# Three lanes of attention blocks instead of two, with more probability and transposed tiles

## The chip, the core and the metric

The kernel runs on one core of a Trainium2 chip. The metric is the device time of one launch in microseconds (us), median of several runs; lower is better. A core has a matrix engine (TensorE, PE in the rows; its weight loads are PEld), a vector engine (VectorE, DVE), an activation engine (ScalarE, ACT), a general engine (GpSimd, POOL) and a queue that issues DMA transfers (SyncE, SP). Each takes its instructions in the order in which they were written for it; between engines they wait on semaphores.

## What is computed

Two layers on 1024 tokens of width 1024: an even layer (RWKV and DeltaNet heads), then an odd layer with chunked attention; each also has an MLP and a gated embedding. All is in 32-bit floats, and products are made three times with a high and a low part of each operand. The change touches the attention of the odd layer alone:

```python
def chunk_band_attention(h, w_qkv, q_g, k_g, rel_bias):     # 16 heads of 64, chunks of 64
    qkv = (h @ w_qkv).reshape(bsz, seq, 3, C_HEADS, C_HEAD_DIM)
    q = rmsnorm(qkv[:, :, 0], q_g) * (C_HEAD_DIM ** -0.5)
    k = rmsnorm(qkv[:, :, 1], k_g)
    v = qkv[:, :, 2]
    ...
    def one_chunk(c):                  # a chunk sees itself and the 8 chunks before it
        s = jnp.einsum('bqhd,bkhd->bhqk', q_c, k_b).astype(jnp.float32) + bias
        s = jnp.where(valid, s, -jnp.inf)
        prob = jax.nn.softmax(s, -1).astype(v.dtype)
        return jnp.einsum('bhqk,bkhd->bqhd', prob, v_b)
```

## The kernel before

The attention is cut into 16 steps (8 pairs of heads, each in two halves of 512 queries), and a step into 4 blocks: 2 heads by 2 blocks of 256 queries, 64 blocks in all. One block (`attn_block`, line 1745) goes through these stations:

- Scores, for each of its two tiles of 128 queries: TensorE writes the near keys, which have a bias that depends on distance, into a bank `sn` of its accumulation memory (PSUM; two such banks) and the far keys into `sf` (one bank). VectorE adds the bias tile `toep` and takes the maximum (line 1795, into the probability tile `pb`), reduces `sf` (L1803) and joins the maxima (L1804); ScalarE takes the exponentials (L1805, L1808); VectorE makes the reciprocal of the sum (L1811); ScalarE scales `pb` with it (L1812). There are four `pb` tiles.
- Transposition: TensorE turns `pb` piece by piece into a bank `pt` (two banks). ScalarE casts it into the high part of a tile `ptile` (L317), VectorE subtracts to get the low part (L318). There are three `ptile` tiles.
- Values: TensorE multiplies `ptile` with the values `vs` into the bank `po` (one bank). After a head's second block, ScalarE copies and VectorE adds one half to the other (L1853, L1854), and `y` is stored.

Around this, `attn_ins` makes the q, k, v products of later steps (`dps<-wq,act`, 24 matmuls of 384 columns for each of 64 tiles of tokens, two banks), and after the last step it goes on with the output projection; `attn_norms` normalizes and transposes q and k of a step.

A planner in the program (`run`, line 112) sets the order in which all this is written: every generator is a lane, and the one whose next piece is due first goes next, by a table of delays (`LAT`). Two of the lanes are `attn_lane`; both draw blocks from one list of jobs, so two blocks are under way. A block's values must follow those of the block before it (`("pv", job - 1)`). The tile framework then orders the instructions of each engine within its own limits, and makes an instruction wait when its tile is still in use.

GpSimd squares q and k (L1711) and, when the first block of a head of a new pair is written, subtracts a number from that head's bias tile `toep` and masks a corner of it (L1753, L1754). The bias tiles come by DMA into three buffers (L1679).

Of the kernel before, what the change touches and what calls it, by code (L numbers as in the profile page):

```python
# [8 lines left out]
F32 = mybir.dt.float32  # L9
F32R = mybir.dt.float32r  # L10
I32 = mybir.dt.int32
AF = mybir.ActivationFunctionType
ALU = mybir.AluOpType
# [4 lines left out]
P = 128  # L18
# [3 lines left out]
HB = 512  # L22
NT = T // P
C = 128
NEG = -1.0e30
# [79 lines left out]
class Trunk:  # L105
# [1470 lines left out]
    def layer1_in(self):  # L1576
        nc, tc, a = self.nc, self.tc, self.a
        with ExitStack() as es:
            self.psm = es.enter_context(self.pool("psml1", space=PSUM))
            wp = self.wp = es.enter_context(self.pool("l1a", 2))  # L1580
            self.wr = es.enter_context(self.pool("l1wr", 2))
            self.w1 = es.enter_context(self.pool("l1w1"))
            l1 = es.enter_context(self.pool("l1", 2))
            self.sm = es.enter_context(self.pool("sml1", 2))
            self.yd = [[self.dr.tile([P, HB], F32, tag=f"yd{k}{hf}", name="yd") for hf in range(2)] for k in range(NK)]
            rbl = l1.tile([P, 16], F32, tag="rbl", name="rbl", bufs=1)
            nc.sync.dma_start(out=rbl, in_=a["rb_last"].rearrange("(o c) -> o c", o=1).broadcast_to((P, 16)))

            steps = [(pr, hf) for pr in range(8) for hf in range(2)]
            self.st = {}  # L1590

            self.ql = [[pool.tile([P, HB], F32R, tag=tag, name="Ql", bufs=1) for pool, tag in
                        ((self.accp, f"acc{e}"), (l1, f"Ql{e}"))] for e in range(2)]
            jobs = iter([(s, h, b) for s in range(16) for h in range(2) for b in range(2)])
            self.run([self.attn_lane(steps, jobs, l1, rbl) for _ in range(2)] + [self.attn_norms(steps, l1), self.attn_ins(steps, l1)])

    def attn_ins(self, steps, l1):
        kv = {}
# [31 lines left out]
        yield from self.out_early(1, self.xd, lambda q: act([P, 2, 2, HB], F32R), xt, load_w,  # L1630
                                  [("at", 14), ("at", 14), ("at", 14), ("at", 15)])

    def attn_norms(self, steps, l1):
        K = []
        for s, (pr, hf) in enumerate(steps):
            yield ("qk", s)
            if s >= 2:
                yield ("at", s - 2)
            yield from self.attn_norm(s, self.st[s], l1)
            K = K[-1:] if hf else []  # L1640
            K = K + [self.st[s]["k"]]
            self.st[s]["K"] = K
            self.mark(("in", s), self.lat["norm"])

    def attn_lane(self, steps, jobs, l1, rbl):

        for s, h, b in jobs:
            yield ("in", s)
            yield from self.attn_block(s, *steps[s], h, b, l1, rbl)

    def weights3(self, odd):

# [89 lines left out]
            st[nm] = F  # L1742
            yield "attn_norm0"

    def attn_block(self, s, pr, hf, h, blk, l1, rbl):

        nc, psm, sm = self.nc, self.psm, self.sm
        V, A, G = nc.vector, nc.scalar, nc.gpsimd
        st = self.st[s]
        m0 = 4 * hf + 2 * blk  # L1750
        if hf == 0 and blk == 0:
            t = st["toep"][h]
            G.tensor_scalar(t, t, rbl[:, 2 * pr + h:2 * pr + h + 1], None, op0=ALU.subtract)  # L1753
            G.memset(t[0:64, 320:384], NEG)  # L1754
        hs = slice(64 * h, 64 * h + 64)
        Q, Ql, K, vs, toep = st["Q"], st["Ql"], st["K"], st["vs"], st["toep"][h]

        def score(ps, m, j0, n):
            qs = slice((m % 4) * P, (m % 4) * P + P)
            o = 0  # L1760
            while o < n:
                j = j0 + o
                e = min(n - o, 4 - j % 4)
                ks = slice((j % 4) * P, (j % 4 + e) * P)
                k = K[j // 4]
                self.mm(ps[:, o * P:(o + e) * P], Q[:, h, qs], k[:, h, ks], start=True, stop=False)
                self.mm(ps[:, o * P:(o + e) * P], Ql[h][:, qs], k[:, h, ks], start=False, stop=True)
                o += e
# [16 lines left out]
        for m in (m0, m0 + 1):  # L1785
            n0 = max(0, m - 2)
            nn = m - n0 + 1
            f0 = max(0, m - 4)
            nf = n0 - f0
            pn = psm.tile([P, HB], F32, tag="sn", name="sn", bufs=2)  # L1790
            score(pn[:, 0:nn * P], m, n0, nn)
            mx = sm.tile([P, 4], F32, tag="mx", name="mx", bufs=4)
            pb = self.wp.tile([P, 5 * P], F32, tag="pb", name="pb", bufs=4)
            S = pb[:, nf * P:(nf + nn) * P]
            V.tensor_tensor_reduce(S, pn[:, 0:nn * P], toep[:, (3 - nn) * P:], op0=ALU.add, op1=ALU.max,  # L1795
                                   scale=1.0, scalar=NEG, accum_out=mx[:, 0:1])
            l = sm.tile([P, 4], F32, tag="l", name="l", bufs=4)
            if nf:
                pf = psm.tile([P, HB], F32, tag="sf", name="sf")
                score(pf[:, 0:nf * P], m, f0, nf)  # L1800
                if m >= 4:
                    V.memset(pf[64:128, 0:64], NEG)
                V.reduce_max(mx[:, 1:2], pf[:, 0:nf * P], axis=AX.X)  # L1803
                V.tensor_scalar(mx[:, 2:3], mx[:, 0:1], mx[:, 1:2], -1.0, op0=ALU.max, op1=ALU.mult)  # L1804
                A.activation(pb[:, 0:nf * P], pf[:, 0:nf * P], AF.Exp, bias=mx[:, 2:3], accum_out=l[:, 1:2])  # L1805
            else:
                V.tensor_scalar(mx[:, 2:3], mx[:, 0:1], -1.0, None, op0=ALU.mult)
            A.activation(S, S, AF.Exp, bias=mx[:, 2:3], accum_out=l[:, 0:1])  # L1808
            if nf:
                V.tensor_tensor(l[:, 0:1], l[:, 0:1], l[:, 1:2], op=ALU.add)  # L1810
            V.reciprocal(l[:, 2:3], l[:, 0:1])  # L1811
            A.activation(pb[:, 0:(nf + nn) * P], pb[:, 0:(nf + nn) * P], AF.Copy, scale=l[:, 2:3])  # L1812
            probs.append((pb, f0))
            yield "attn_block0"
# [9 lines left out]
        for b in range(bank + 1):  # L1824
            pt = psm.tile([P, HB], F32, tag="pt", name="pt", bufs=2)
            for j, (bb, o, c0, c1) in place.items():
                if bb != b:
                    continue
                for e in range(2):
                    if c0 <= 128 * e < c1:  # L1830
                        pb, f0 = probs[e]
                        self.tr(pt[:, o + 128 * e - c0:o + 128 * e - c0 + P],
                                            pb[:, (j - f0) * P:(j - f0 + 1) * P], self.ident)
            t = self.wp.tile([P, 2, HB], F32R, tag="ptile", name="ptile", bufs=3)
            self.split_scaled(t, pt[:, 0:used[b]], None, slice(0, used[b]))
            pts.append(t)
            yield "attn_block2"
# [3 lines left out]
        for j, c0, c1 in segs:  # L1841
            b, o, _, _ = place[j]
# [111 lines left out]
```

## Time and profile before

| | us |
|---|---|
| median of 3 runs | 3196.68 (3195.02 to 3198.12) |
| the profiled execution | 3200.01 |
| its span, first to last instruction | 3198.3 |
| TensorE busy in the span | 3102.1 (97%) |
| VectorE, ScalarE, GpSimd busy | 2013.2, 1384.2, 531.5 |

The profile is of one execution; the span starts and ends with an instruction, and the 1.7 us beyond it lie around the program. Times in rows are us from the span's start, unless ns is written. A busy TensorE is not a TensorE at its peak: matmuls overlap, and the pace is read from one start to the next. The attention stands between about 1772 and 2396 us. "PEclk" is the share of TensorE's full clock that the chip granted in a stretch.

### The profile page before, as it was taken

Reading aid. Unit: us, or ns where it says so; the run is one execution under the profiler, and the core shown is the slowest. Engines: PE = TensorE matmul, PEld = TensorE weight load, DVE = VectorE, ACT = ScalarE, POOL = GpSimd, SP = SyncE. Lnnn points to the kernel's source line nnn. Section 1 sums busy time; section 2 is a strip of 40 time slices with the busy share of each in tenths; the row PEclk is TensorE's granted clock in tenths of the full one; section 3 lists DMA queues with packets and bytes.
Section 4 is the critical chain, followed back from the end, with each engine's and each line's share of the span. In section 5 each row is a group of like instructions: output and inputs, shape, how many; then the busy total and the mean of one; then the engine's idle time right before and its main releaser. Section 6 shows DMA issues by size and latency. Waiting matters only on the chain.

```text
span 3198.3 us, 46044 instructions
## 1 busy us (share of the span) xinstructions
PE 3102.1 (97%) x17576; PEld 2565.6 (80%) x17576; DVE 2013.2 (63%) x4020; ACT 1384.2 (43%) x2608; POOL 531.5 (17%) x978
## 2 busy tenths in 40 slices
PE   7999999999999999999999898999899999999999
PEld 5777777777777888888888888988778888888887
DVE  6566675556748666655546576776768666655552
ACT  4333333334326555322123477777756555312121
POOL 6334442433410000000004211010110000000002
PEclk8999899999899999999999999999999999999999
DMA  3322112212325433523213210110156433522213
GB/s 120 94 63 60 47 46 67 70 61 70 129 95 194 155 119 108 192 93 106 92 51 128 70 36 32 45 41 16 69 177 209 150 121 109 185 105 92 106 47 105
DMA packets 144716, 309.60 MB, mean 97 GB/s; under 512 B 40944, under 2 KB 43120, under 8 KB 144496
## 3 DMA queue, kind: packets, MB, share of 16 engines
q1 hardware_dynamic: 126064, 273.10, 25.6%
q10 hardware_dynamic: 18432, 33.56, 2.7%
q8 instruction: 138, 2.26, 0.3%
q14 instruction: 82, 0.67, 0.1%
HBM read 232.16 MB, written 74.45 MB: 96 GB/s over the span
## 4 chain that ended last, share of the span: by engine, by line
PE 85%; DVE 7%; ACT 3%; DMA 2%; issue 1%; POOL 0%; SPq 0%; ACTq 0%; DVEq 0%; POOLq 0%
PE dps L161 70%; PE ch L161 3%; PE iz L161 2%; PE pm L161 2%; PE tp L161 1%; PE po L161 1%; PE py L161 1%; DVE ptile L318 1%; PE pt L165 1%; DMA wraw<-in_w_qkv 1%; PE sn L161 1%; PE pp L161 1%; DVE pb L1795 1%; PE sc L161 1%; ACT pb L1808 1%
## 5 line engine op out<-in xcount | busy, mean ns | idle before, releaser
L161 PE MATMUL dps<-r,act 128*128 128x512 f32 x3528 | 824.4, 392 | 0.0
L161 PEld LDWEIGHTS dps<-r,act 128*128 128x128 f32 x3528 | 662.1, 188 | 145.7
L161 PE MATMUL dps<-xg,whi 128*128 128x512 f32 x1280 | 438.2, 418 | 11.7 <-ACT xg L320 7.3
L161 PE MATMUL dps<-late,act 128*128 128x512 f32 x1536 | 352.9, 391 | 0.0
L161 PEld LDWEIGHTS dps<-late,act 128*128 128x128 f32 x1536 | 288.4, 188 | 63.1
L161 PE MATMUL dps<-wq,act 128*128 128x384 f32 x1536 | 304.8, 344 | 5.8 <-DVE vs L1704 3.1
L1452 POOL TENSOR_TENSOR pn<-pn,prs 128x512 f32<-128x512 f32 x32 | 45.5, 1426 | 1590.7 <-ACT prs L354 1496.3
L161 PEld LDWEIGHTS dps<-xg,whi 128*128 128x128 f32 x1280 | 248.4, 199 | 75.2 <-issue 10.7
L161 PEld LDWEIGHTS dps<-wq,act 128*128 128x128 f32 x1536 | 265.6, 191 | 10.4 <-DVE vs L1704 5.1
L161 PE MATMUL dps<-xg,wlo 128*128 128x512 f32 x640 | 266.4, 416 | 3.1 <-DVE wlo L277 3.1
L1328 DVE TENSOR_TENSOR late<-late,dps 128x512 f32<-128x512 f32 x224 | 152.9, 685 | 150.1 <-PE dps L161 119.2
L1427 DVE TENSOR_TENSOR xw<-xw,dps 128x512 f32<-128x512 f32 x192 | 131.5, 685 | 148.4 <-PE dps L161 145.5
L1226 ACT CAST act<-act 128x1024 fp32r<-128x1024 f32 (+1 forms) x99 | 94.8, 964 | 285.2 <-DMA act<-in_w 124.2
L1226 ACT CAST act<-late 128x512 fp32r<-128x512 f32 x210 | 124.5, 618 | 135.9 <-PE dps L161 117.0
L1227 DVE TENSOR_TENSOR act<-late,act 128x512 fp32r<-128x512 f32 x210 | 139.9, 687 | 26.1 <-ACT act L1226 25.9
L161 PEld LDWEIGHTS dps<-xg,wlo 128*128 128x128 f32 x640 | 126.9, 198 | 34.1 <-issue 4.8
L161 PE MATMUL dps<-xw,act 128*128 128x512 f32 x576 | 138.9, 392 | 0.0
L276 ACT CAST whi<-wraw 128x1024 fp32r<-128x1024 f32 x78 | 81.7, 1047 | 124.2 <-PE dps L161 74.4
L161 PEld LDWEIGHTS dps<-xw,act 128*128 128x128 f32 x576 | 108.1, 188 | 24.1
L1227 DVE TENSOR_TENSOR act<-act 128x1024 fp32r<-128x1024 f32 (+1 forms) x99 | 109.9, 1115 | 21.0 <-ACT act L1226 19.8
L161 PE MATMUL po<-ptile,vs 128*128 128x256 f32 (+1 forms) x576 | 104.9, 297 | 17.1 <-DVE ptile L318 7.7
L277 DVE TENSOR_TENSOR wlo<-wraw,whi 128x1024 fp32r<-128x1024 f32 x78 | 101.4, 1301 | 25.6 <-ACT whi L276 25.6
(472 smaller groups left out, 5369.4 us busy)
## 6 DMA issues: line engine op xcount, KB each, us to landing
act<-in_w SPq DMA_DIRECT2D x68, 512.0 KB
hd<-late ACTq DMA_DIRECT2D x128, 256.0 KB
late<-in_w SPq DMA_DIRECT2D x60, 512.0 KB
wraw<-in_w_in SPq DMA_DIRECT2D x56, 512.0 KB
act<-hd SPq DMA_DIRECT2D x56, 512.0 KB
wraw<-in_w_out SPq DMA_DIRECT2D x21, 512.0 KB
wraw<-in_w_qkv SPq DMA_DIRECT2D x21, 512.0 KB
pn<-pnd SPq DMA_DIRECT2D x32, 256.0 KB
```

The lines of the kernel that those rows point to most:

```text
L161: return self.nc.tensor.matmul(out, lhsT, rhs, start=start, stop=stop)
L165: return self.nc.tensor.transpose(out, in_, ident)
L276: nc.scalar.copy(hi, raw)
L277: nc.vector.tensor_tensor(lo, raw, hi.bitcast(F32), op=ALU.subtract)
L318: nc.vector.tensor_tensor(dst[:, 1, sl], src, dst[:, 0, sl].bitcast(F32), op=ALU.subtract)
L1226: A.copy(hi, s)
L1227: V.tensor_tensor(lo, s, hi.bitcast(F32), op=ALU.subtract)
L1328: V.tensor_tensor(r, t, u, op=ALU.add)
L1427: V.tensor_tensor(x[n][:, sl], x[n][:, sl], ps, op=ALU.add)
L1452: G.tensor_tensor(pn, pn, prs[:, sl], op=ALU.mult)
L1795: V.tensor_tensor_reduce(S, pn[:, 0:nn * P], toep[:, (3 - nn) * P:], op0=ALU.add, op1=ALU.max, scale=1.0, scalar=NEG, accum_out=mx[:, 0:1])
L1808: A.activation(S, S, AF.Exp, bias=mx[:, 2:3], accum_out=l[:, 0:1])
```

## The change

Three lanes draw from the list of blocks. The `pb` tiles go from 4 to 6, the `ptile` tiles from 3 to 4. The memory for that comes from a reserve for descriptors of dynamic DMAs, set to 1024 bytes. The work on the two bias tiles of a pair moves from the first block of each head to `attn_norms`, where both are done when the pair's first step is normalized. Nothing is computed that was not computed before, and no instruction is added or removed.

```diff
-            self.run([self.attn_lane(steps, jobs, l1, rbl) for _ in range(2)] + [self.attn_norms(steps, l1), self.attn_ins(steps, l1)])
+            self.run([self.attn_lane(steps, jobs, l1) for _ in range(3)] + [self.attn_norms(steps, l1, rbl), self.attn_ins(steps, l1)])
...
             yield from self.attn_norm(s, self.st[s], l1)
+            for h in range(0 if hf else 2):
+                t = self.st[s]["toep"][h]
+                self.nc.gpsimd.tensor_scalar(t, t, rbl[:, s + h:s + h + 1], None, op0=ALU.subtract)
+                self.nc.gpsimd.memset(t[0:64, 320:384], NEG)
...
-        if hf == 0 and blk == 0:
-            t = st["toep"][h]
-            G.tensor_scalar(t, t, rbl[:, 2 * pr + h:2 * pr + h + 1], None, op0=ALU.subtract)
-            G.memset(t[0:64, 320:384], NEG)
...
-            pb = self.wp.tile([P, 5 * P], F32, tag="pb", name="pb", bufs=4)
+            pb = self.wp.tile([P, 5 * P], F32, tag="pb", name="pb", bufs=6)
...
-            t = self.wp.tile([P, 2, HB], F32R, tag="ptile", name="ptile", bufs=3)
+            t = self.wp.tile([P, 2, HB], F32R, tag="ptile", name="ptile", bufs=4)
...
-    nc = bacc.Bacc("TRN2", target_bir_lowering=False, num_devices=1)
+    nc = bacc.Bacc("TRN2", target_bir_lowering=False, num_devices=1,
+                   dynamic_dma_scratch_size=1024)
```

The other lines of the diff pass `rbl` to `attn_norms` instead of `attn_block`.

How this moves instructions is shown at two places. The first is TensorE at the last block of the sixth step (`pt` is a bank of transposed probabilities, `po` the bank of value products, `sn` and `sf` scores of other blocks). Before:

```order
L161 MATMUL sf<-F_18069,F_18119 128x128
L161 MATMUL sf<-F_18069,Ql 128x128
L165 MATMUL pt<-ident,pb 128x128 x6
L161 MATMUL po<-ptile,vs 128x256
L165 MATMUL pt<-ident,pb 128x128 x2
L161 MATMUL po<-ptile,vs 128x256 x7
L161 MATMUL po<-ptile,vs 128x128
L165 MATMUL pt<-ident,pb 128x128 x3
```

The first value product stands right behind the transpositions that make its tile. The same block on TensorE after the change:

```order
L165 MATMUL pt<-ident,pb 128x128 x4
L161 MATMUL sn<-F_18100,F_18119 128x128
L161 MATMUL sn<-F_18100,Ql 128x128
L161 MATMUL po<-ptile,vs 128x128
L161 MATMUL sn<-F_18100,F_18119 128x256
L161 MATMUL sn<-F_18100,Ql 128x256
L161 MATMUL po<-ptile,vs 128x128 x3
L165 MATMUL pt<-ident,pb 128x128 x4
L161 MATMUL sf<-F_18100,F_18119 128x128
L161 MATMUL sf<-F_18100,Ql 128x128
L161 MATMUL po<-ptile,vs 128x256
L165 MATMUL pt<-ident,pb 128x128 x2
```

The first four transpositions belong to the block; the 128-column value products behind them are still the block before's. Scores, those products and four more transpositions now stand between the first bank and the first product of its tile (`po` with 256 columns).

The second place is GpSimd, in the stretch where the bias tile of the second head of the fourth pair is made ready (`toep_17528` before, `toep_17552` after; `sq` is the squaring of q and k). Before:

```order
L1711 TENSOR_TENSOR sq_17848<-qk_17530 128x512
L1711 TENSOR_TENSOR sq_17851<-qk_17530 128x512
L1753 TENSOR_SCALAR toep_17528<-toep_17528,rbl_15492 128x384
L1754 MEMSET toep_17528 64x64
L1711 TENSOR_TENSOR sq_18326<-qk_17867 128x512
L1711 TENSOR_TENSOR sq_18329<-qk_17867 128x512
```

After, with the change's own line numbers:

```order
L1715 TENSOR_TENSOR sq_17908<-qk_17554 128x512
L1715 TENSOR_TENSOR sq_17911<-qk_17554 128x512
L1642 TENSOR_SCALAR toep_17552<-toep_17552,rbl_15492 128x384
L1715 TENSOR_TENSOR sq_18400<-qk_17927 128x512
L1643 MEMSET toep_17552 64x64
L1715 TENSOR_TENSOR sq_18403<-qk_17927 128x512
```

The subtraction keeps its place ahead of the next step's squares; the masking slips behind the first of them.

## Rows read from the trace of the kernel before

**Rows 1.** Busy time by stretch: attention, then rest; PE, PEld, DVE, ACT, POOL, PEclk, DMA.
```profile
1800.00:2396.00 596.00, 548.80 (x3365) 505.08 (x3364) 420.89 (x1325) 428.43 (x996) 70.89 (x69) 0.97 0.18 58
2396.00:3190.00 794.00, 794.00 (x3479) 650.22 (x3478) 477.20 (x654) 285.95 (x431) 21.67 (x16) 1.00 0.35 123
```

**Rows 2.** Who TensorE waited for, 1800 to 2396: us in total, times, longest.
```profile
PE po L161 <- DVE ptile L318: 7.7, 12, 1.6
PE po L161 <- ACT ptile L317: 6.4, 10, 1.8
PE pt L165 <- ACT pb L1812: 6.1, 9, 1.8
PE pt L165 <- DVE ptile L318: 4.8, 12, 1.0
PE sf L161 <- ACT pb L1805: 3.8, 7, 1.3
```

**Rows 3.** Timeline of all engines at one block: start, us, instruction, idle before it.
```profile
2019.13 0.88 PE L165 MATMUL pt<-ident,pb 128*128 128x128 f32 x6
...
2020.03 1.05 ACT L317 CAST ptile<-pt 128x512 fp32r<-128x512 f32 x2
2020.62 0.69 DVE L318 TENSOR_TENSOR ptile<-pt,ptile 128x512 fp32r<-128x512 f32 x1 [1.37 <-ACT ptile L317]
2020.64 0.38 PE L161 MATMUL po<-ptile,vs 128*128 128x256 f32 x1 [0.64 <-ACT ptile L317]
2021.23 0.68 DVE L1712 TENSOR_REDUCE ss<-sq 128x8 f32<-128x512 f32 x1
2021.37 0.44 PE L165 MATMUL pt<-ident,pb 128*128 128x128 f32 x2 [0.34 <-DVE ptile L318]
...
2021.82 0.68 DVE L318 TENSOR_TENSOR ptile<-pt,ptile 128x512 fp32r<-128x512 f32 x1
...
2022.56 0.68 PE L161 MATMUL po<-ptile,vs 128*128 128x256 f32 x4 [0.28 <-DVE ptile L318]
```

**Rows 4.** Lines by shape, 1800 to 2396: count, busy us, mean ns, idle before.
```profile
L318 DVE TENSOR_TENSOR ptile<-pt,ptile 128x512 fp32r<-128x512 f32 x80 | 53.3, 683 | 12.3 <-ACT ptile L317 11.5
L317 ACT CAST ptile<-pt 128x512 fp32r<-128x512 f32 x80 | 44.3, 587 | 10.1 <-PE pt L165 9.7
L1812 ACT ACTIVATE pb<-pb,l 128x640 f32<-128x640 f32 x64 | 53.2, 832 | 16.2 <-DVE l L1811 14.3 <-DVE ss L1713 1.6
L1808 ACT ACTIVATE pb<-pb,mx 128x384 f32<-128x384 f32 x96 | 58.6, 610 | 2.7 <-DVE mx L1807 2.7
L1805 ACT ACTIVATE pb<-sf,mx 128x256 f32<-128x256 f32 x64 | 30.4, 475 | 47.6 <-DVE mx L1804 47.4
L1803 DVE TENSOR_REDUCE mx<-sf 128x1 f32<-128x256 f32 x64 | 26.6, 416 | 0.9
L1854 DVE TENSOR_TENSOR y<-po,otmp 64x512 f32<-64x512 f32 x32 | 22.0, 686 | 4.1 <-ACT otmp L1853 3.6
L1853 ACT COPY otmp<-po 64x512 f32<-64x512 f32 x32 | 18.6, 581 | 2.9 <-PE po L161 2.1
L1795 DVE CUSTOM_DVE_ANT_0 pb<-sn,toep 128x384 f32<-128x384 f32 x96 | 51.6, 551 | 11.0 <-PE pt L165 8.5 <-PE sn L161 1.6
```

**Rows 5.** TensorE's timeline between two stalls, for its pace.
```profile
2269.82 3.46 PE L161 MATMUL dps<-wq,act 128*128 128x384 f32 x19
2273.12 0.45 PE L161 MATMUL po<-ptile,vs 128*128 128x128 f32 x3
...
2278.77 0.28 PE L161 MATMUL sf<-F,F 128*128 128x256 f32 x1
2278.88 0.28 PE L161 MATMUL sf<-F,Ql 128*128 128x256 f32 x1
```

**Rows 6.** Waits of VectorE and GpSimd, 1800 to 2396: us in total, times, longest.
```profile
DVE pb L1795 <- PE pt L165: 11.2, 11, 2.7
POOL toep L1753 <- DMA toep<-in_rb: 38.4, 7, 8.2
```

More of the change, by code (lines that the diff above doesn't have):

```diff
@@ L1631, in attn_ins, with attn_norms @@
                                   [("at", 14), ("at", 14), ("at", 14), ("at", 15)])
-    def attn_norms(self, steps, l1):
+    def attn_norms(self, steps, l1, rbl):
         K = []
@@ L1643, in attn_norms, with attn_lane @@
             self.mark(("in", s), self.lat["norm"])
-    def attn_lane(self, steps, jobs, l1, rbl):
+    def attn_lane(self, steps, jobs, l1):
         for s, h, b in jobs:
             yield ("in", s)
-            yield from self.attn_block(s, *steps[s], h, b, l1, rbl)
+            yield from self.attn_block(s, *steps[s], h, b, l1)
     def weights3(self, odd):
@@ L1743, in attn_norm, with attn_block @@
             yield "attn_norm0"
-    def attn_block(self, s, pr, hf, h, blk, l1, rbl):
+    def attn_block(self, s, pr, hf, h, blk, l1):
         nc, psm, sm = self.nc, self.psm, self.sm
```

## The prediction

> **What bounds the kernel now.** I read the busy time by stretch first. From 2396 us on TensorE is busy 794.00 of 794.00 us at the full clock; in the attention it is busy 548.80 of 596.00 us at 0.97 of the clock [rows 1]. So TensorE bounds the whole program, nothing behind 2396 us can hide or eat what the attention saves, and the attention holds 596.00 − 548.80 = 47.2 us of idle TensorE. The clock adds something: at 1.00 instead of 0.97 the stretch would be about 0.03 × 596 = 18 us shorter. VectorE (420.89 us) and ScalarE (428.43 us) are busy 71 and 72% of it: not the bound, but not far away.
>
> Next, the waits: the longest ones are value products `po` that wait for `ptile`, 7.7 + 6.4 us, then transpositions that wait for a scaled `pb` (6.1 us) or for a free `pt` bank (4.8 us), then `sf` (3.8 us) [rows 2]. No wait is long; 1.8 us is the longest of these. The timeline of one block shows what they are: six transpositions in a row, and then nothing that TensorE could do while ScalarE casts and VectorE subtracts; it stands for 0.64, 0.34 and 0.28 us in one block [rows 3]. A reader should see there that TensorE's rows follow too closely on what they need, and that one subtraction stood behind another instruction of VectorE (the reduction at 2021.23).
>
> **The change, part by part.** Nothing is added or removed, so its worth is the distance that the new order puts between a producer on TensorE and the row that needs the answer.
>
> How I count: along TensorE's rows, in both orders, each row at its pace in the trace: (2273.12 − 2269.82)/19 = 0.174 us for 384 columns, 0.11 us for 256 [rows 5], the rest likewise. From the last row of a producer to the first row that needs it is the distance. The price is what stands between on the other engines. Where the price is longer, the difference is a shortage.
>
> 1. Transposed tile to value product. Price: 587 ns cast + 683 ns subtraction = 1.27 us for 512 columns [rows 4], in proportion for narrower ones. Of 144 tiles, 40 are short before, by 23.1 us together; after, 29, by 13.0 us. **−10.1 us.** The block shown ahead is one: TensorE has 0.25 us of other work behind its first bank before, and 1.05 us after.
> 2. The next use of a `pt` bank, at the same price: 28 of 142 short by 11.1 us; after, 16 by 7.1 us. **−4.0 us.**
> 3. Scores to transposition. The four long passes are 416 + 475 + 610 + 832 ns = 2.33 us [rows 4]; with some six short ones between I take 3.4 us: 9 of 128 short by 7.1 us, after 5 by 4.0. **−3.1 us.** At 2.33 us alone nearly nothing is short in either order, so this term is 0 to −3 us, and more if the lanes' queues make the price longer.
> 4. The banks that the third lane has to share. `sn` (551 ns [rows 4]): 1.2 us of shortage goes to 0. `po`, one bank, 581 + 686 ns [rows 4]: 0.5 us becomes 2.4. `sf`, one bank, at the same 1.27 us: 1.0 becomes 2.5. The two banks of q, k, v: 5.1 becomes 6.5. Together **+3.6 us**: here the third lane costs.
>
> The sum goes from 49.1 us to 35.5 us of shortage. Before, 47.2 us of idle were measured, so the count is true to 4%, and I take −13.6 × 47.2/49.1 = **−13.1 us**.
>
> 5. The clock. It is not granted in full where TensorE pauses often (0.97 against 1.00 [rows 1]). I let its 18 us shrink with the shortages, by 13.6/49.1 = 28%: **−5 us**. Ends: 0 if the same low stretches stay, −18 if all go.
> 6. More `pb` tiles. VectorE waited 11.2 us for a `pb` tile that was still being transposed [rows 6]. It is an engine with slack, so I count nothing of it beyond the terms above; at most those 11.2 us.
> 7. The bias tiles. The subtraction and the masking move on GpSimd, and the DMA that feeds them waits for the same release as before: three buffers still. GpSimd already waits 38.4 us for these DMAs [rows 6] with nobody delayed. After the change the next step's squares follow the same subtraction, but at three of seven pairs only some 2.5 to 3.7 us of TensorE's rows stand between the release and the squares' source, where it was 6 to 7. VectorE's reduction of the squares, and what is queued behind it, could wait for that. Bounds: nothing, or the longest wait in that row for each, 3 × 8.2 = 25 us; near nothing, since the reduction stands behind other work of VectorE: **+1 us**. The SP queue keeps the order of loads and stores but for a store of `y` that goes ahead of a bias tile, which costs nothing: the projections' weights are issued a step early.
>
> Total: −13.1 − 5 + 1 = −17.1, so **−17 us**. Against the profiled execution, 3200.0 us, that is 3183 us; that execution was 3.3 us above the median of the runs (3196.7), so I give 3196.7 − 17 = 3180 us.
>
> **The rivals.**
>
> A. *The lanes stand in each other's queue (slower).* Place: ScalarE's casts and VectorE's subtractions, which follow in order behind another lane's softmax. Price: I lengthen each of the chains above by a delay, once (the softmax twice). At 0.15 us the shortages of the new order are 49.3 us, those of the old one without it: this is the point from which it decides. At 0.3 us they are 64.9: +15.8 × 0.96 = +15 us, with the clock in the same proportion +6, so 3196.7 + 21 = 3218 us. For it: both engines are above 70% [rows 1], one pass there takes up to 832 ns [rows 4], and the block's second subtraction stood behind a reduction of 0.68 us [rows 3]. Against it: the work of both engines stays the same, and of VectorE's 80 reductions of far scores only 13 stand behind a row whose scores TensorE makes later, where it was 25.
>
> B. *Only the buffers count (no change).* The stalls then come from tiles and banks that are not free, the banks stay as they are, and what is bought is VectorE's 11.2 us [rows 6]. Of TensorE's idle 7.7 + 4.8 of 47.2 us is put down to VectorE [rows 2], so 3 us of them arrive: 3194 us. The Trainium skill has this as a rule (Perfetto Trace Analysis, Optimization Strategy): the same gap repeating on the engine that should be saturated can mean that memory for the next tile ran out. Where the rows speak against it: the longest waits are for a tile being written, not for a free one.
>
> C. *There is more to gain than TensorE's idle time.* The weight loads idle 596.00 − 505.08 = 90.9 us in the stretch [rows 1], and the stalls spoil the overlap of load and product around them. The same 28% of that is −25 us, with the clock and the bias tiles −29: 3168 us. Against it: in the rest, without any stall, the loads idle too (650.22 of 794.00 us busy [rows 1]). The Trainium skill would judge by this number (Perfetto Trace Analysis, Identifying the Most-Contended Engine): a matmul's busy share is a bad measure of how near TensorE is to its limit, that of the weight loads a good one.
>
> That three lanes run no further ahead than two is excluded by the order: scores of up to eight tiles lie ahead of their transpositions instead of six.
>
> **How the numbers follow.** About 0.2%, 6.4 us, is what a measurement of this kernel can tell from no change. Forecast (−17, between −8 and −25): 0.50. C: 0.17. B: 0.19. A: 0.14. The forecast's own low edge gives a little to "same" as B its edge to "faster"; so faster 0.67, same 0.19, slower 0.14. The range leaves out A beyond its start and the far end of C: 3163 to 3200 us. Its low end is C with 5 us more from the clock; its high end is B with 3 us for the bias tiles on top and the spread of the runs.
>
> **What would show it.** Right: in the attention's stretch TensorE's idle time falls from 47 to some 34 us and most of the fall is in `po` waiting for `ptile`; the granted clock rises from 0.97; waits for `po` and `sf` banks grow by some us; GpSimd's wait for the bias DMAs delays no reduction. A shows as longer waits for `ptile` although the distances grew, B as the same waits without VectorE's 11.2 us, C as idle weight loads that shrink by more than TensorE's idle. I am wrong if TensorE's idle in the stretch does not fall by 8 us or more, or if the time behind the attention changes.

## The result

The changed kernel takes 3211.5 us (median of 6 runs, 3205.9 to 3224.4), the kernel before 3196.6 us beside it: a ratio of 1.0048, with a 95% interval of 1.0032 to 1.0064. It is 15 us slower where 17 us less were forecast.

The profiled execution of the change took 3224.4 us, the longest of the six. A second profile, taken later, is of an execution of 3212.3 us; where the two differ, both numbers are given. One execution of pad_before, a kernel of the experiments, took 5874 us, its eleven others 3199 to 3210; it was the profiled one, so it is left out of that kernel's ratio and its trace is not used. The first view is the busy time by stretch of the changed kernel; its columns are those of [rows 1].

```profile
1800.00:2396.00 596.00, 541.22 (x3308) 504.83 (x3308) 414.65 (x1316) 423.81 (x990) 68.46 (x69) 0.95 0.16 54
2396.00:3190.00 794.00, 788.68 (x3445) 645.06 (x3444) 479.58 (x653) 288.40 (x433) 16.22 (x12) 1.00 0.35 124
```

Against [rows 1], TensorE's idle time in the attention rose from 596.00 − 548.80 = 47.2 to 596.00 − 541.22 = 54.8 us (56.0 in the second profile). The granted clock fell from 0.97 to 0.95 (0.97 in the second). And 794.00 − 788.68 = 5.3 us of idle stand behind 2396 us, where there was none.

Next, whom TensorE waits for in the attention of the changed kernel (us in total, times, longest):

```profile
PE pt L165 <- DVE ptile L318: 8.7, 13, 1.9
PE dps L161 <- DVE F L1744: 8.7, 4, 3.3
PE sf L161 <- ACT pb L1805: 8.7, 9, 2.8
PE po L161 <- ACT ptile L317: 5.5, 7, 1.3
PE pt L165 <- DVE F L1744: 2.8, 1, 2.8
...
PE po L161 <- DVE ptile L318: 2.0, 5, 0.6
...
PE pt L165 <- ACT pb L1812: 1.6, 4, 0.8
```

Held against [rows 2], two waits went as forecast: `po` for `ptile` from 14.1 to 7.5 us, `pt` for `pb` from 6.1 to 1.6. Three waits for a bank grew: `pt` from 4.8 to 8.7 us, `sf` from 3.8 to 8.7, and the waits for L1744 to 8.7 + 2.8. In the kernel before, that line is L1740:

```profile
PE dps L161 <- DVE F L1740: 1.8, 4, 0.5
```

L1744 writes the low parts of the normalized q and k (`Ql`, `F`); it is the last to read the bank into which q or k was transposed. Behind it waits a product of a later step that wants the same bank.

One such place, on TensorE's timeline of the changed kernel (`dps<-ident,qk` are the transpositions of q or k):

```profile
2057.00 0.60 PE L165 MATMUL dps<-ident,qk 128*128 128x128 f32 x4
2057.35 0.37 PE L161 MATMUL sf<-F,F 128*128 128x256 f32 x1
...
2058.20 0.33 PE L161 MATMUL sn<-F,Ql 128*128 128x384 f32 x1
2058.37 0.66 PE L165 MATMUL dps<-ident,qk 128*128 128x128 f32 x4
2058.86 0.38 PE L165 MATMUL pt<-ident,pb 128*128 128x128 f32 x2
2059.72 0.38 PE L161 MATMUL sf<-F,F 128*128 128x256 f32 x1 [0.47 <-ACT pb L1805]
2059.94 0.28 PE L161 MATMUL sf<-F,Ql 128*128 128x256 f32 x1
2063.24 0.98 PE L161 MATMUL dps<-wq,act 128*128 128x384 f32 x2 [3.02 <-DVE F L1744]
```

ScalarE in the same stretch, and then VectorE's two instructions on the first of the two banks:

```profile
2058.54 0.67 ACT L1741 ACTIVATE F<-dps,vecs 64x512 fp32r<-64x512 f32 x1
2059.11 0.46 ACT L1805 ACTIVATE pb<-sf,mx 128x256 f32<-128x256 f32 x1
...
2059.56 0.62 ACT L1808 ACTIVATE pb<-pb,mx 128x384 f32<-128x384 f32 x1
...
2060.16 0.68 ACT L1741 ACTIVATE F<-dps,d_qg 64x512 fp32r<-64x512 f32 x1
2060.85 0.68 ACT L1743 ACTIVATE F<-dps,d_qg 64x512 fp32r<-64x512 f32 x1
2061.56 0.68 ACT L1741 ACTIVATE F<-dps,vecs 64x512 fp32r<-64x512 f32 x1
```

```profile
2059.54 0.74 DVE L1744 SCALAR_TENSOR_TENSOR F<-dps,vecs,F 64x512 fp32r<-64x512 f32 x1
...
2062.34 0.76 DVE L1744 SCALAR_TENSOR_TENSOR F<-dps,vecs,F 64x512 fp32r<-64x512 f32 x1
```

The first bank was full at 2057.60 and free at 2063.10 us, 5.5 us later. The four passes over it (0.67 and 0.68 us on ScalarE, 0.74 and 0.76 on VectorE) need far less; between the first half and the second, ScalarE's queue holds two softmax passes and two passes on the other bank. On TensorE the rows that stand between are done at 2060.22 us, 2.6 us after the bank was full, and then it stands for 3.0 us. No value product is among these rows: the lanes are at their scores or at transpositions.

Last, the place behind the attention. First what TensorE and SP wait for there in the changed kernel; then SP's timeline, where the first loads of the output projection's next weights are issued after the change; then the same row of the kernel before.

```profile
PE dps L161 <- ACT late L1226: 5.3, 1, 5.3
...
SPq L1230 <- PE dps L161: 8.2, 1, 8.2
```

```profile
2423.82 0.81 SPq L1230 DMA_DIRECT2D late<-in_w_out  x2
```

```profile
2399.82 0.85 SPq L1230 DMA_DIRECT2D late<-in_w_out  x2
```

The load waits 8.2 us for a product, and TensorE then waits 5.3 us for what was loaded. In the program's memory map the reason is plain. The tile into which the next weights are split starts at byte 84256 of a partition before, just where the weights `wq` of the last 48 attention products end. The larger `pb` and `ptile` tiles push `wq` up by 9216 bytes in relation to it: after the change `wq` holds bytes 53536 to 78112 and the new tile starts at 68896. So the loads must now wait for the last product that reads `wq`.

### The profile page after: what moved, and what is told of

Same layout as the page of the kernel before. It is cut to its first block, busy times and chain, and to the rows that moved or that the text cites. A ratio compares the mean times of both kernels' runs of the same rounds, so it can differ in the third digit from the quotient of the medians.

```text
span 3222.3 us, 46042 instructions
## 1 busy us (share of the span) xinstructions
PE 3116.9 (97%) x17576; PEld 2581.9 (80%) x17576; DVE 2014.9 (63%) x4020; ACT 1385.1 (43%) x2608; POOL 527.7 (16%) x978
## 4 chain that ended last, share of the span: by engine, by line
PE 88%; DVE 5%; ACT 4%; DMA 1%; issue 1%; POOL 0%; SPq 0%; DVEq 0%; ACTq 0%; POOLq 0%
PE dps L161 72%; PE ch L161 3%; PE iz L161 2%; PE pm L161 2%; PE po L161 2%; PE tp L161 1%; PE py L161 1%; PE sn L161 1%; PE pt L165 1%; ACT pb L1808 1%; PE pp L161 1%; PE sc L161 1%; ACT ptile L317 0%; ACT pb L1812 0%; PE st L161 0%
## 5 line engine op out<-in xcount | busy, mean ns | idle before, releaser
L161 PEld LDWEIGHTS dps<-xg,whi 128*128 128x128 f32 x1280 | 247.9, 198 | 74.0 <-issue 11.1
L161 PEld LDWEIGHTS dps<-wq,act 128*128 128x128 f32 x1536 | 277.6, 198 | 16.8 <-issue 8.4
L1332 ACT ACTIVATE late<-late 128x512 f32<-128x512 f32 x128 | 80.2, 628 | 84.1 <-DVE late L1328 76.3
```

Of the source, the lines that this page charges most:

```text
L161: return self.nc.tensor.matmul(out, lhsT, rhs, start=start, stop=stop)
L1332: A.activation(t, t, AF.Relu)
```

## Experiments

Each kernel is compared with the kernel before, run beside it on the same chip; rows with another "before" are from another occasion, so kernels are held against each other by their ratios. Lines of code that are not shown are those of the kernel named.

| kernel | lanes | tiles | us | before | ratio, 95% interval |
|---|---|---|---|---|---|
| the change | 3 | new | 3211.5 | 3196.6 | 1.0048 (1.0032 to 1.0064) |
| late_apart | 3 | new, weights apart | 3207.1 | 3195.5 | 1.0035 (1.0021 to 1.0048) |
| pad_before | 2 | old, moved by 9216 bytes | 3203.7 | 3195.5 | 1.0024 (1.0010 to 1.0038) |
| two_lanes | 2 | new | 3201.3 | 3195.5 | 1.0011 (1.0001 to 1.0022) |
| two_toep | 2 | old, bias work moved | 3194.1 | 3195.5 | 1.0000 (0.9988 to 1.0013) |
| two_late_apart | 2 | new, weights apart | 3188.8 | 3194.5 | 0.9982 (0.9972 to 0.9992) |
| stag4 | 3, starts 4 us apart | new, weights apart | 3193.2 | 3194.5 | 0.9993 (0.9983 to 1.0002) |
| stag7 | 3, starts 7 us apart | new, weights apart | 3185.7 | 3194.5 | 0.9977 (0.9968 to 0.9986) |
| sf_apart | 3, far scores 2 us apart | new, weights apart | 3201.6 | 3194.5 | 1.0016 (1.0006 to 1.0026) |
| two_pb6 | 2 | `pb` 6, `ptile` 3, weights apart | 3191.8 | 3197.1 | 0.9985 (0.9975 to 0.9996) |
| two_stag7 | 2, starts 7 us apart | new, weights apart | 3186.5 | 3197.1 | 0.9968 (0.9957 to 0.9978) |
| before_stag7 | 2, starts 7 us apart | old | 3212.6 | 3197.1 | 1.0049 (1.0036 to 1.0061) |

### Where the new weights lie

**late_apart.** The changed kernel with a gap, so that the next weights lie behind `wq` again:

```diff
+            if last:
+                es.enter_context(self.pool("gap")).tile([P, 2304], F32, tag="gap", name="gap")
             late = es.enter_context(self.pool("late1")) if last else self.rx
```

> The changed kernel with an empty tile of 9216 bytes a partition ahead of the tiles in which the next stage (output projection) gets its weights, so that they no longer lie over the weights that the last attention products read. TensorE's order in the attention is that of the changed kernel. Theory 'room' (the larger tiles moved the projection's weights under the next stage's loads): the wait of 5.3 us at 2429 us goes, and with it the low clock behind it, 2.7 us: 3211.5 - 8 = 3203.5 us, and the loads are issued before the last of the 48 products of the second half ends. Theory 'lanes' (all of the loss is in the attention, from the third lane): 3211 us, the stall appears elsewhere.

The two rows are the stretch behind the attention, 2396 to 2440 us, of the change and of this kernel:

```profile
2396.00:2440.00 44.00, 38.69 (x158) 30.55 (x157) 24.24 (x34) 18.09 (x28) 0.00 (x0) 0.92 0.61 208
```

```profile
2396.00:2440.00 44.00, 44.00 (x191) 35.59 (x190) 28.61 (x41) 22.70 (x34) 0.00 (x0) 1.00 0.70 238
```

The wait is gone, and the clock is whole there, where 0.08 of 44 us, 3.5 us, was lost. By the ratios 4 of the 15 us went, less than the 8 expected; their intervals overlap, so this size is loose.

**pad_before.** The other way round: the kernel before, with `wq` pushed up, and with the change's DMA reserve.

```diff
+            wp.tile([P, 2304], F32, tag="pad", name="pad", bufs=1)
             self.wr = es.enter_context(self.pool("l1wr", 2))
```

> The kernel before (two lanes, old tiles) with an unused tile of 9216 bytes a partition in the pool that the change made larger by as much, and the DMA reserve of the change. TensorE's order is that of before. Theory 'room': the load of the next stage's weights, issued at 2399.8 us before, waits for the last of the 48 products, to about 2407.6 us, and TensorE stands for 5 us behind it, with some low clock: 3196.6 + 5 to 8 = 3202 to 3205 us. Theory 'lanes': no change, 3196.6 us.

It became 8 us slower in 3195.5, with no lane and no used tile added (the reserve by itself costs nothing: two_toep below has it too). With two lanes and the new tiles the same gap was worth 0.0029 of the time, or 9 us (two_lanes against two_late_apart, whose intervals do not touch). So the place of the weights costs 4 to 9 us of the 15: 5 us of waiting and, by the estimate above, up to 3.5 us for the low clock beside it.

### The lanes, the tiles and the bias tiles

**two_lanes** is the change with two lanes:

```diff
-            self.run([self.attn_lane(steps, jobs, l1) for _ in range(3)] + [self.attn_norms(steps, l1, rbl), self.attn_ins(steps, l1)])
+            self.run([self.attn_lane(steps, jobs, l1) for _ in range(2)] + [self.attn_norms(steps, l1, rbl), self.attn_ins(steps, l1)])
```

**two_toep** is two_lanes with the old number of tiles, so that of the change only the work on the bias tiles and the DMA reserve are left:

```diff
-            pb = self.wp.tile([P, 5 * P], F32, tag="pb", name="pb", bufs=6)
+            pb = self.wp.tile([P, 5 * P], F32, tag="pb", name="pb", bufs=4)
...
-            t = self.wp.tile([P, 2, HB], F32R, tag="ptile", name="ptile", bufs=4)
+            t = self.wp.tile([P, 2, HB], F32R, tag="ptile", name="ptile", bufs=3)
```

> The changed kernel with two lanes instead of three (more tiles, bias tiles in the normalization, as in the change). Theory 'lanes': the new waits for the transposes' banks and for sf go, the larger tiles help a little, only the wait behind the attention stays: 3196.6 + 8 - 5 = 3199 us, range 3194 to 3204. Theory 'tiles' (the order that the larger tiles bring costs as much with two lanes): 3208 to 3214 us as the changed kernel.

> Two lanes, the old number of tiles, the DMA reserve of the change, and the work on the bias tiles moved as in the change. TensorE's order is that of before. If GpSimd's squares behind the moved work delay VectorE's reductions and TensorE: up to 10 us slower, 3197 to 3207 us. If that work has slack: 3196.6 us within 3 us.

Two lanes with all the rest are 12 us faster than three, though they have the wait behind the attention as well:

```profile
PE dps L161 <- ACT late L1226: 5.2, 1, 5.2
```

The moved bias work costs and gains nothing that can be seen.

**two_late_apart** has both edits, the gap of late_apart and the two lanes of two_lanes.

> Two lanes with the change's tiles, and the empty tile of 9216 bytes that keeps the next stage's weights off the old ones. Theory 'room plus lanes': the two costs add. Two lanes gave 3201.3 us with the wait behind the attention (5.2 us in its profile); without it 3201.3 - 4.4 to 8 = 3193 to 3197 us, so 10 to 14 us faster than three lanes without it (3207.1). Rival (the third lane costs nothing by itself, its runs only differ by chance of the order): 3203 to 3207 us.

It is faster than the kernel before, by 0.18%, and faster than late_apart, from which it differs in the third lane alone, by 0.0053 of the time, or 17 us, where 10 to 14 were expected. So the new tiles gain 6 us, and the third lane costs 17. Most of this is idle TensorE in the attention, 596.00 − 538.91 = 57.1 us in late_apart and 41.9 here; first the row of late_apart, then that of this kernel:

```profile
1800.00:2396.00 596.00, 538.91 (x3311) 502.21 (x3311) 417.36 (x1316) 423.02 (x988) 68.01 (x69) 0.96 0.17 56
```

```profile
1800.00:2396.00 596.00, 554.07 (x3393) 514.38 (x3393) 420.97 (x1327) 429.72 (x999) 71.14 (x69) 0.96 0.19 64
```

The waits at the same banks, two rows of the view that was shown above for the change, first of late_apart:

```profile
PE sf L161 <- ACT pb L1807: 10.3, 9, 2.8
...
PE dps L161 <- DVE F L1746: 8.1, 4, 3.2
```

The same two of this kernel:

```profile
PE sf L161 <- ACT pb L1807: 4.2, 7, 1.0
...
PE dps L161 <- DVE F L1746: 1.1, 5, 0.4
```

And TensorE behind the same kind of transposition:

```profile
2053.30 0.60 PE L165 MATMUL dps<-ident,qk 128*128 128x128 f32 x4
2053.65 0.31 PE L161 MATMUL sf<-F,F 128*128 128x128 f32 x1
...
2054.57 0.39 PE L161 MATMUL po<-ptile,vs 128*128 128x256 f32 x1 [0.28 <-ACT ptile L317]
2055.89 0.41 PE L165 MATMUL pt<-ident,pb 128*128 128x128 f32 x2 [0.93 <-DVE ptile L318]
2056.05 1.05 PE L161 MATMUL po<-ptile,vs 128*128 128x256 f32 x7
```

Here one lane is at its values while the other is at its scores, so there are eight value products to do while the banks are held.

### Why the third lane costs

**stag4.** If it is the starting together that costs, three lanes must be cheap once they start apart. The lanes get one more rule:

```diff
             yield ("in", s)
+            n = 4 * s + 2 * h + b
+            if n:
+                yield ("go", n - 1)
+            self.mark(("go", n), 4.0)
             yield from self.attn_block(s, *steps[s], h, b, l1)
```

> Three lanes, the change's tiles, weights kept apart, and one rule more in the planner: a block's first scores are written at least 4.0 us (planner's time) after those of the block before it. Theory 'bunching' (three lanes wait for the same step, start together, and the two banks of the transposed q and k are wanted again after 1.2 us of products, where they are held for 3.2 to 7.3): the loss at those banks falls from 12 us to some 5, the rest stays: 3207.1 - 7 = 3200 us, range 3195 to 3203. Rival (the third lane costs through the queues of ScalarE and VectorE, wherever its blocks start): 3207 us within 3.

```profile
PE sf L161 <- ACT pb L1811: 4.0, 6, 1.0
...
PE dps L161 <- DVE F L1750: 1.1, 5, 0.3
```

With three lanes both waits are back where two lanes have them, and 0.0042 of the time comes back, 13 of the 17 us, more than was expected. ScalarE's and VectorE's work, the lanes and the tiles are the same as in late_apart; only when the blocks begin differs. That excludes the rival as it was put, that the queues cost wherever the blocks start. Nor did the q and k banks come free sooner: from the last product into such a bank to the end of its last reader it takes a median of 5.0 us here and 5.1 in late_apart. The order changed: counted at the prediction's paces, the earliest that another product wants such a bank again is after 2.7 us of products, where it was 1.2.

One thing is not separated. By the planner's own time, worked out by running its `run` for each kernel, 25 of 63 blocks of the change start within 2 us of the one ahead, none in stag4; but three blocks are also under way less often, 33% of the time instead of 54. Whether starting together costs, or having three under way, these runs do not tell.

**stag7** changes one number of stag4:

```diff
-            self.mark(("go", n), 4.0)
+            self.mark(("go", n), 7.0)
```

> As the kernel with 4.0 us between the starts of blocks, with 7.0 us (a block takes TensorE some 10 us with its share of other products). Theory 'bunching': the distances after which sf, the q and k banks and the pt banks are wanted again are all longer than in the change; of the losses at sf (15 us) and at the q and k banks (12 us) about half goes, of those at pt and po a third: 3207.1 - 13 to - 20 = 3187 to 3194 us, with less low clock at the lower end. Rival (queues): 3207 us within 4.

It is 0.23% faster than the kernel before, 0.58% faster than late_apart. The forecast of 3187 to 3194 us was a little high. By the planner's time no three blocks are under way here, so it is three lanes in name only.

**two_stag7** is stag7 with the edit of two_lanes.

> Two lanes, the change's tiles, weights kept apart, 7.0 us between the starts of blocks. Theory 'bunching' says that the third lane only starts blocks too close: with 7.0 us between starts it has next to nothing to do, and two lanes give the same as three: 3185.7 us within 3. Rival (a third lane is worth something once it is spread): 3 us slower or more, 3189 to 3195 us.

Two lanes do as well as three (3186.5 and 3185.7 us), so a third lane is worth nothing once starts are this far apart. This version beats both kernels, by 0.32% the one before. Its attention, in the columns of [rows 1]:

```profile
1800.00:2396.00 596.00, 556.21 (x3394) 512.66 (x3394) 425.92 (x1331) 431.99 (x1003) 70.59 (x69) 0.98 0.20 66
```

Idle is 39.8 us where it was 47.2, and the clock 0.98.

**sf_apart** is late_apart with far scores kept apart instead of blocks:

```diff
+            self.nsf, self.tq = -1, None
...
+            if nf:
+                k = self.nsf = self.nsf + 1
+                if k:
+                    yield ("sf", k - 1)
             pn = psm.tile([P, HB], F32, tag="sn", name="sn", bufs=2)
...
                 score(pf[:, 0:nf * P], m, f0, nf)
+                self.mark(("sf", k), 2.0)
```

> Three lanes, the change's tiles, weights kept apart, and a rule in the planner that far scores are written at least 2.0 us after the far scores before them. Theory 'bunching', at the one sf bank: the loss at sf falls from 15 us to some 11, with 2 us more at the q and k banks and at po: 3207.1 - 4 to - 6 = 3201 to 3203 us. Rival (queues): 3207 us within 3.

The time is the expected one, the reason is not:

```profile
PE sf L161 <- ACT pb L1813: 11.5, 6, 2.8
...
PE dps L161 <- DVE F L1747: 4.3, 3, 1.9
```

The wait for `sf` did not shrink (11.5 us, where late_apart has 10.3); the one for the q and k banks did (4.3 for 8.1 us). The profile is of this kernel's fastest execution, 3192.5 us, so these numbers are rather low for it. How much of the 17 us is due to `sf` alone stays open.

**two_pb6** is two_late_apart with three `ptile` tiles:

```diff
-            t = self.wp.tile([P, 2, HB], F32R, tag="ptile", name="ptile", bufs=4)
+            t = self.wp.tile([P, 2, HB], F32R, tag="ptile", name="ptile", bufs=3)
```

> Two lanes, six probability tiles, but three transposed tiles as before, weights kept apart. TensorE's order is that of the kernel with two lanes and all the new tiles (3188.8 us). Theory 'order by probability tiles' (what the two lanes gain comes from the order that two more probability tiles allow): 3188.8 us within 3. Rival (the fourth transposed tile is what lets ScalarE and VectorE run ahead): near 3194.5 us, as before.

It is as fast as with four, within the intervals. What the new tiles gain comes from the `pb` tiles: with six of them the framework writes another order for TensorE, with four it writes that of the kernel before.

**before_stag7** is the kernel before with the rule of stag7 in its `attn_lane`, and nothing else.

> The kernel before (two lanes, four probability and three transposed tiles) with 7.0 us between the starts of blocks and nothing else. Its order has longer distances at sf, po and pt than before, but the q and k banks are wanted again after 1.5 us of products in some places, where they were after 2.7. Theory 'bunching': gains and losses nearly cancel, 3194.5 us within 5; so the larger tiles are needed for the gain of the kernel with three spread lanes. Rival (spacing alone makes the gain): 3186 us.

```profile
PE pt L165 <- ACT pb L1816: 16.9, 13, 3.0
PE po L161 <- ACT ptile L317: 16.0, 13, 2.4
```

It is 15 us slower, not equal, and waits for the q and k banks are not why (0.6 us for L1744): the waits that grew are those for `pb` and `ptile` being written, 33 us together. Both theories missed this; it shows that the spacing needs the new tiles. Its trace shows where most of these waits come from. First TensorE, then ScalarE:

```profile
2053.77 0.87 PE L165 MATMUL pt<-ident,pb 128*128 128x128 f32 x6
...
2057.41 0.39 PE L161 MATMUL po<-ptile,vs 128*128 128x256 f32 x1 [2.37 <-ACT ptile L317]
```

```profile
2054.67 0.68 ACT L1741 ACTIVATE F<-dps,d_qg 64x512 fp32r<-64x512 f32 x1
2055.36 0.68 ACT L1743 ACTIVATE F<-dps,d_qg 64x512 fp32r<-64x512 f32 x1
2056.07 0.68 ACT L1741 ACTIVATE F<-dps,vecs 64x512 fp32r<-64x512 f32 x1
2056.77 1.07 ACT L317 CAST ptile<-pt 128x512 fp32r<-128x512 f32 x2
```

The transpositions are done at 2054.64 us, and the cast starts 2.1 us later, behind three passes on q and k in ScalarE's queue. Four waits of 2.37 us have this form, and at four more, of 3.02 us, three such passes stand ahead of the scaling of `pb`: 21.6 of the 33 us. So the queue of ScalarE can cost as rival A of the prediction had it, in this order if not in the change's.

**again** is the changed kernel once more, for a second profile.

> The changed kernel once more, for a second profile. Theory 'room plus bunching': TensorE waits again some 5 us for the weights behind the attention and some 10 us for banks of transposed q and k; one time between 3204 and 3216 us. If these waits are missing or stand elsewhere, they belong to one execution and not to the kernel.

Both waits are there: 5.2 us behind the attention, and 8.6 + 2.8 us for L1744. The time was 3212.3 us.

## Why the prediction was wrong

**Term 1 (value products, −10.1 us) was right.** The wait fell by 6.6 us in the first profile, to 7.5, and by 8.9 in the second. But it is not the third lane that brings it: with two lanes and the new tiles (two_late_apart) the same wait is 4.9 + 1.7 = 6.6 us. **Term 3** (−3.1) was right too: −4.5.

**Term 4 (+3.6 us) is the step that failed, and term 2 (−4.0) with it.** They price a bank by the bare passes over it, 1.27 us for `pt` and `sf`; for q, k and v the price is not given, but 5.1 to 6.5 us of shortage. But a bank is held until its last reader has come up in the queue of ScalarE or VectorE. From the trace of before, the time from the last product into a bank to the end of its last reader had a median of 2.2 us for `pt` (144 banks), 3.85 us for `sf` (80 banks), and of 6.2 us for transposed q and k (32 banks), of which none was held for less than 3.2. With 3.2 us for the latter, the count that the prediction made gives 1.5 us of shortage before and 11.1 after; the waits for L1744 went from 1.8 to 11.5. With two lanes and the new tiles it gives 1.6, and 1.1 were measured. For `pt` at 2.2 us it gives 43.5 and 42.2, so no gain in place of −4.0; measured were +3.9. For `sf`, at 3.8 us, 32.5 becomes 42.2; measured were +4.9. So in place of term 4's +3.6 us, the rows for `sf` and L1744 alone grew by 4.9 + 9.7 = 14.6 us.

These counts were made after the result, and they are estimates. For q and k they use the shortest hold, for the others the median, and at the median they give far more shortage than was waited for (43.5 and 32.5 us before, where [rows 2] has 4.8 and 3.8). A shortage is also no wait where TensorE stands for something else first, as in before_stag7: its expectation has the q and k banks wanted again after 1.5 us, and 0.6 us were waited for L1744. That banks were held for longer than their passes is measured; how much a place will cost does not follow from the hold alone.

The count's agreement with the idle time before, to 4%, was chance, as its terms show: it had 23.1 us where [rows 2] has 14.1 (`po` for `ptile`), 11.1 where it has 4.8 (`pt` for its bank) and 1.0 where it has 3.8 (`sf`).

**The place of the tiles was missing.** The prediction gave the memory no term and took it that nothing behind 2396 us would change. It named a changed time there as a sign of being wrong, and that sign came: 4 to 9 us. So did its other one, an idle time in the attention that does not fall: it rose by 7.6 us.

**Term 5 (the clock, −5 us) had the wrong sign.** The mean granted clock was 0.9743 over 30 runs of the kernel before and 0.9718 over 6 of the change; of 3200 us that is an estimated 8 us more, probably too much (see the sum below). In the trace of before, each of the seven low stretches from 1760 to 2440 us (41 us together) begins in or behind stalls of 1.3 to 6.4 us in all. The change makes more of such places (2.8 to 3.3 us at one bank): its two profiles have 13 and 12 low stretches there, of 75 and 58 us together.

**Terms 6 and 7.** The `pb` tiles, counted at nothing, gain 5 us with two lanes (two_pb6); they do it by the order that they allow, which the count in terms 1 to 4 held already. The bias tiles cost nothing, as the +1 had it.

**The rivals.** A had the right sign and nearly the right size (+21 us), but another mechanism: it made the chains longer in the new order. They are not; from the last transposition into a bank to a finished `ptile` it takes 2.59 us on the average before and 2.53 after. The queues are long in both kernels; the new order comes back to the q and k banks sooner. B, that only the tiles count, describes the two-lane kernel: 0.9982 is 3191 us, where B said 3194. C, that more than TensorE's idle time is to be gained, did not come: the weight loads idled 90.9 us in the attention before and 596.00 − 504.83 = 91.2 after. The rule that stood beside B (the Trainium skill, Perfetto Trace Analysis, Optimization Strategy: the same gap coming again can mean that memory for the next tile is short) is borne out in part: two more `pb` tiles gained 5 us, through another order of TensorE's rows. Another of its rules speaks for what failed (the Trainium skill, Perfetto Trace Analysis, Optimizing Tensor Performance: rotate independent groups through different banks, so that one is emptied while the next is filled). The trace agrees and adds that two banks in turn were too few where each was held for 3.2 us or more and the product that wanted one came after 2.6 (2057.60 to 2060.22 us).

**The sum.** By the steps between the ratios: the new tiles −6 us (the moved bias work, at 0, in them), the third lane +17, the place of the weights +4. These steps follow one path from the kernel before to the change, so they must add up to the +15 us that were measured; with two lanes the place of the weights costs 9 us, and then the third lane 12. The traces give a check of their own: 7.6 us more idle time in the attention (8.8 in the second profile) and 5.3 us behind it are 13 to 14 us. Of the 15 little is left for the clock, so the estimate of 8 us looks too high.

## What to carry to other kernels

Look at how long a buffer is held, from the last write to the last read in the trace, queues included, and not only at the passes over it; then ask after how much work the new order comes back to it. More lanes want the same few banks at the same time: here two lanes at their best did as well as three, and spreading the starts of blocks gained more than a lane, though only with the new tiles. A larger tile also moves what lies behind it, so look in the memory map at what the next stage loads into.

## What was not expected of the hardware

The clock does not follow the sum of the idle time. First the attention in stag4, then in stag7:

```profile
1800.00:2396.00 596.00, 554.05 (x3395) 516.50 (x3394) 421.44 (x1330) 427.69 (x998) 72.61 (x70) 0.96 0.18 59
```

```profile
1800.00:2396.00 596.00, 556.46 (x3395) 512.81 (x3396) 426.42 (x1330) 431.50 (x1001) 69.92 (x69) 0.98 0.20 66
```

stag4 has 42.0 us of idle TensorE and stag7 39.5, nearly the same; but the low clock (0.50 of the full one, 1.2 instead of 2.4 GHz) was granted for 48 us of this stretch in the one and for 27 us in the other. The mean clocks over their runs agree, 0.9709 and 0.9759. By the same estimate as above that would be 16 us, but their times differ by 7.5, so this estimate is too high. What in the pattern of the stalls decides the clock is not shown.
